# Attention logits in two row halves of the array, with the key sums and the mask in a bias tile made on GpSimd

## The chip, the cores and the metric

The kernel runs on one core of one Trainium2 chip. The metric is device time in microseconds of one launch. A profiled execution has a span (from the first to the last instruction of the program) and a time of its own, which is a little longer.

## What is computed

A small decoder trunk of two layers for 256 tokens of width 1024: a recurrent layer (RG-LRU), then an attention layer, each with two half-step feed-forward networks (hidden width 2816) around it and RMS norms. All data are float32. The part that matters here is the attention, with 16 heads of width 64 and a running sum `c` of forget gates per head and token:

```python
log_f = jax.nn.log_sigmoid((hn @ w_f + b_f).astype(jnp.float32))
c = jnp.cumsum(log_f, axis=1).transpose(0, 2, 1)
...
logits = jnp.einsum('bhqd,bhkd->bhqk', q[:, :, q0:end], k[:, :, :end]).astype(jnp.float32)
logits = logits + c[:, :, q0:end, None] - c[:, :, None, :end]
logits = jnp.where(kpos[None, :] <= qpos[:, None], logits, -jnp.inf)
p = jax.nn.softmax(logits, axis=-1).astype(v.dtype)
```

## The kernel before

The 256 tokens are two row tiles of 128, called `t` = 0 and 1. Every matrix product runs as three products in fp32r (a 32-bit format of TensorE): each weight tile is loaded (`raw`), split on ScalarE into an upper part `whi` (line 173) and on VectorE into the rest `wlo` (line 177), and `mm3` (lines 183 to 185) adds hi x hi, hi x lo and lo x hi into a PSUM bank `mm`. Weights come through a list of items in the order of use. An item has a `prep` (load and split) and a `work` for each row tile. Up to nine split items lie ready, so the preps run ahead of the work. `ahead(i, fn)` runs a function just before the prep of item `i`; `defer(n, fn)` runs one after `n` more steps of work.

The program order on TensorE is written by hand. VectorE, ScalarE, GpSimd (POOL) and the DMA queues are ordered by the framework's scheduler, which takes instructions under `high_priority` first and keeps the order only of those marked `keep_in_program_order`.

Stages in order: feed-forward, recurrent layer, feed-forward, keys and values with the forget gates (`post_f`, `running`), feed-forward of layer 2 (its first four items run ahead of the keys and values), attention, feed-forward. Inside a feed-forward network a gate tile `sil` and a product `prod` are made for 512 hidden columns at a time. A DMA on the SP queue moves `prod` to a tile `prr` (line 515), and TensorE transposes that some steps later (line 525). The last 256 columns (`alone`) take `prr` from the two buffers of tag `sil`. The 22 down-projection items follow.

Logits before: queries and keys are stored transposed, one head at a time, in `qT` and `kT` with 66 rows: 64 of the head, and two that carry the sums, so that one product over 66 rows gives q.k + c(query) - c(key). `heads_T` transposes two heads at once and copies the lower 64 rows with ScalarE and the upper 64 with VectorE, so that both start at row 0. In float32 a product takes two passes in the trace.

The attention stage is a hand-written order, `ATT_ORDER` (line 1125). A digit is one half-item of the projections for that row tile. A letter with a digit is a step of the attention for that row tile: `l` logits of one group (four heads at t=0 with 128 keys, two at t=1 with 256 keys; one 512-wide bank of tag `gt`, which has two), `n` normalisation, `t` transposes of the probabilities (line 1084), `v` the product with the values in two column halves (line 1098). In `l`, TensorE makes the logits (line 1063), VectorE adds the causal mask (1064) and takes the negated maximum (1066), and ScalarE takes the exponential with a row sum (1071). In `n`, VectorE inverts the sum (1077) and multiplies (1078). There are four groups at t=0 and eight at t=1.

Of the kernel before, what the change touches and what calls it, by code (L numbers as in the profile page):

```python
# [23 lines left out]
NRT = 11  # L24
NH = 16
HD = 64
HA = HD + 2
EPS = 1e-6
RAW = 5
WB = 9  # L30
# [3 lines left out]
NEG = -1e30  # L34
# [10 lines left out]
def trunk_kernel(ctx: ExitStack, tc: tile.TileContext, A: dict, out: bass.AP):  # L45
    nc = tc.nc
# [5 lines left out]
    hpool = ctx.enter_context(tc.tile_pool(name="h", bufs=1))  # L52
    spool = ctx.enter_context(tc.tile_pool(name="small", bufs=4))
    psum = ctx.enter_context(tc.tile_pool(name="psum", bufs=1, space=bass.MemoryType.PSUM))

    uid = [0]

    def nm(s):
        uid[0] += 1
        return f"{s}_{uid[0]}"  # L60
# [20 lines left out]
    def defer(n, fn):  # L81
        pend.append([n, fn])
# [474 lines left out]
    def std_dests(gi):  # L557
        return lambda t: [main_dest(gi, t)]


    pools = {}
# [345 lines left out]
    kv = {}  # L907
# [9 lines left out]

    def kv_tiles():
        lp = ctx.enter_context(tc.tile_pool(name="kv", bufs=1, reuse_waits="tile"))
        kv["kT"] = lp.tile([HA, NH, S], F32, name="kT")  # L920
# [3 lines left out]
        kv["c"] = [lp.tile([NH, P], F32, name=f"c{t}") for t in range(2)]  # L924
        kv["bfb"] = lp.tile([P, NH], F32, name="bfb")
        for n in ("triu", "mone", "cmask"):
            kv[n] = lp.tile([P, P], F32, name=n)

    def kv_constants():

        keep = tc.keep_in_program_order
        triu, cm = kv["triu"], kv["cmask"]
        keep(nc.gpsimd.dma_start(kv["bfb"], A["b_fgate"].partition_broadcast(P)))
        keep(nc.gpsimd.memset(triu, -1.0))
        keep(nc.gpsimd.affine_select(out=triu, in_=triu, compare_op=ALU.is_ge, fill=0.0, base=0,
                                     pattern=[[1, P]], channel_multiplier=-1))
        keep(nc.gpsimd.memset(kv["mone"], -1.0))
        keep(nc.gpsimd.memset(cm, 0.0))
        keep(nc.gpsimd.affine_select(out=cm, in_=cm, compare_op=ALU.is_ge, fill=NEG, base=0,
                                     pattern=[[-1, P]], channel_multiplier=1))  # L940
        keep(nc.gpsimd.memset(kv["kT"][HD:HA, :, :], 1.0))

    def att_rows():

        tc.keep_in_program_order(nc.scalar.activation(warm, mhalf, AF.Exp))
        for t in range(2):
            tc.keep_in_program_order(nc.gpsimd.dma_start(att["q"][t][HD:HD + 1, :, :], kv["c"][t]))
            tc.keep_in_program_order(nc.gpsimd.dma_start(att["q"][t][HD + 1:HA, :, :], kv["mone"][:NH, :]))

    def heads_T(pool, ps, t, n, scale, dst):  # L950

        tok = pool.tile([P, 512], F32, tag="prod", name=nm("htok"), bufs=2)
        with tc.high_priority():
            nc.vector.tensor_scalar(tok, ps, rs[t][:, 0:1], scale, ALU.mult, ALU.mult)

        def turn():
            tp = trbank()
            for j in range(4):
                nc.tensor.transpose(tp[:, j * P:(j + 1) * P], tok[:, j * P:(j + 1) * P], ident)  # L959
            to = dst[:HD, 8 * n:8 * n + 8, :].rearrange("p (a two) b -> p a two b", two=2)  # L960
            with tc.high_priority():
                nc.scalar.activation(to[:, :, 0, :], tp[:HD, :].rearrange("p (a b) -> p a b", a=4), AF.Copy)
                nc.vector.tensor_copy(to[:, :, 1, :], tp[HD:, :].rearrange("p (a b) -> p a b", a=4))
        defer(2, turn)

    def post_k(n):
        return lambda t, ps: heads_T(pools["f"], ps, t, n, 1.0, kv["kT"][:, :, t * P:(t + 1) * P])

    def post_f(t, ps):
        fp = pools["f"]  # L970
# [60 lines left out]
    for n in range(2):  # L1031
# [3 lines left out]
    ffn_items(lambda: pools["f"], A["ffn1_w_gate"][1], A["ffn1_w_up"][1], A["ffn1_w_down"][1], A["ffn1_post_g"][1],  # L1035
              std_dests(GI[("mix", 1)]))
    n_ffn3 = len(items)

    items[n_ffn2:n_kv + 4] = items[n_kv:n_kv + 4] + items[n_ffn2:n_kv]


    att = {}

    def att_tiles():
        ap = pools["a"]
        att["q"] = [ap.tile([HA, NH, P], F32, name=f"qT{t}") for t in range(2)]
        att["oh"] = [ap.tile([P, 8, P], F32R, name=f"oh{t}") for t in range(2)]
        att["ol"] = [ap.tile([P, 8, P], F32R, name=f"ol{t}") for t in range(2)]

    def attention(t):  # L1050

        ap = pools["a"]
        nk = t + 1
        per = 4 // nk
        mask = kv["cmask"].unsqueeze(1).to_broadcast([P, per, P])
        box = {}
        G = NH // per

        def logits(hg):
            hds = range(hg * per, (hg + 1) * per)  # L1060
            ps = gtbank().rearrange("p (a b) -> p a b", a=per)
            for j, hd in enumerate(hds):
                nc.tensor.matmul(ps[:, j, :], att["q"][t][:, hd, :], kv["kT"][:, hd, :nk * P], start=True, stop=True)  # L1063
            nc.vector.tensor_tensor(ps[:, :, t * P:], ps[:, :, t * P:], mask, ALU.add)
            mx = spool.tile([P, 4], F32, tag="mx", name=nm("mx"))
            nc.vector.tensor_reduce(mx[:, :per], ps, AX.X, ALU.max, negate=True)
            if hds[0] % 8 == 0:
                box["sm"] = spool.tile([P, 8], F32, tag="sm", name=nm("sm"))
            pe = ap.tile([P, per, nk * P], F32, tag="pe", name=nm("pe"), bufs=3)
            for j, hd in enumerate(hds):  # L1070
                nc.scalar.activation(pe[:, j, :], ps[:, j, :], AF.Exp, bias=mx[:, j:j + 1],
                                     accum_out=box["sm"][:, hd % 8:hd % 8 + 1])
            box["pe", hg], box["s", hg] = pe, box["sm"][:, hds[0] % 8:hds[0] % 8 + per]

        def norm(hg):
            pe, sm = box["pe", hg], box["s", hg]
# [30 lines left out]
        return {c: [lambda i=i, f=f: f(i) for i in range(G)] for c, f in zip("lntv", (logits, norm, turn, values))}  # L1107

    def post_q(n):
        return lambda t, ps: heads_T(pools["a"], ps, t, n, HD ** -0.5, att["q"][t])  # L1110

    for n in range(2):
        proj_items(A["attn_w_q"][0], n * 512, 512, main_x, post_q(n))
# [246 lines left out]
```

## Time and profile before

| | |
|---|---|
| median of 3 runs | 987.58 us (987.57 to 987.7) |
| the profiled execution | 987.51 us |
| its span | 985.8 us |
| TensorE busy | 978.0 us, 99% |
| VectorE busy | 616.6 us, 63% |
| ScalarE busy | 530.1 us, 54% |
| GpSimd busy | 47.2 us, 5% |
| attention stage, first to last logits | about 734 to 777 us |

A row of the page or of the groups names the line, the engine, the operation, what is written and read (`out<-in`), the shapes and the count, then busy time in us and mean ns of one, then the idle time ahead of it. In a timeline a row has the start in us, the length in us, and then the same names; several neighbours are merged, with their count. PE is TensorE, PEld its weight load, DVE VectorE, ACT ScalarE, POOL GpSimd, SP the engine that issues most DMAs. A matmul's length includes its way through the array, so the distance from one start to the next says what it costs in a stream.

### The profile page before, as it was taken

The page shows a single profiled execution, that of the slowest core. Times are in us where ns is not written, and L with a number is a line of the kernel's source. Part 1 is how long each engine was busy: PE and PEld are TensorE (multiplying, and loading weights), DVE is VectorE, ACT ScalarE, POOL GpSimd, SP SyncE. Part 2 cuts the span into 40 slices and gives each one's busy share as a digit, 9 for nine tenths or more (in the row PEclk, how much of TensorE's full clock was granted, in tenths as well). Part 3 has the DMA queues.
Part 4 walks back from the last instruction along what each step waited for, and adds up shares of the span by engine and source line. Part 5 has one row for each costly group of instructions (what it writes and reads, how often), then busy time and mean ns, then how long its engine had stood idle before and what let it go on. Part 6 is the DMA issues. An engine that isn't in the chain of part 4 may idle for free.

```text
span 985.8 us, 13028 instructions
## 1 busy us (share of the span) xinstructions
PE 978.0 (99%) x4777; PEld 813.4 (83%) x4777; DVE 616.6 (63%) x791; ACT 530.1 (54%) x753; POOL 47.2 (5%) x92
## 2 busy tenths in 40 slices
PE   9999999999999999999999999999999999999997
PEld 6888888898978888888898888888888788888886
DVE  6666554678997555554686655554488876555542
ACT  7545443568986544443564444544366755444431
POOL 2400000100003000000100000000020000000000
PEclk9999999999999999999999999999999999999999
DMA  8787766565346877666567676665552467776631
GB/s 292 263 266 249 222 210 192 158 192 162 117 126 198 241 211 212 217 207 188 131 203 242 186 220 213 214 213 185 190 173 64 123 210 235 213 213 212 205 117 43
DMA packets 99558, 190.45 MB, mean 193 GB/s; under 512 B 12734, under 2 KB 32614, under 8 KB 99494
## 3 DMA queue, kind: packets, MB, share of 16 engines
q1 hardware_dynamic: 98054, 188.95, 61.3%
q8 instruction: 38, 0.62, 0.3%
q10 hardware_dynamic: 608, 0.53, 0.2%
q0 software_dynamic: 832, 0.12, 0.1%
q14 instruction: 26, 0.21, 0.1%
HBM read 176.95 MB, written 1.05 MB: 181 GB/s over the span
## 4 chain that ended last, share of the span: by engine, by line
PE 98%; issue 1%; DVE 1%; ACT 0%; POOL 0%; POOLq 0%; DVEq 0%; ACTq 0%
PE mm L183 29%; PE mm L185 29%; PE mm L184 28%; PE gt L761 2%; PE tr L525 1%; PE mm L1195 1%; PE gt L1063 1%; PE mm L190 1%; PE mm L191 1%; PE mm L192 1%; PE mm L1098 1%; PE tr L1084 1%; PE gt L214 1%; PE tr L127 0%; PE tr L959 0%
## 5 line engine op out<-in xcount | busy, mean ns | idle before, releaser
L177 DVE TENSOR_TENSOR wlo<-raw,whi 128x1024 fp32r<-128x1024 f32 (+5 forms) x329 | 395.3, 1207 | 268.3 <-ACT whi L173 266.1
L173 ACT ACTIVATE whi<-raw 128x1024 fp32r<-128x1024 f32 (+5 forms) x329 | 341.9, 1046 | 314.8 <-PE mm L185 260.2
L183 PE MATMUL mm<-whi,xhi 128*128 128x512 f32 (+1 forms) x768 | 301.2, 392 | 0.0
L185 PE MATMUL mm<-whi,xlo 128*128 128x512 f32 (+1 forms) x768 | 298.2, 388 | 0.3 <-DVE xlo L228 0.3
L184 PE MATMUL mm<-wlo,xhi 128*128 128x512 f32 (+1 forms) x768 | 297.9, 388 | 0.0
L185 PEld LDWEIGHTS mm<-whi,xlo 128*128 128x128 f32 x768 | 144.2, 188 | 30.7 <-DVE xlo L228 0.7
L183 PEld LDWEIGHTS mm<-whi,xhi 128*128 128x128 f32 x768 | 144.2, 188 | 29.4 <-issue 1.3
L184 PEld LDWEIGHTS mm<-wlo,xhi 128*128 128x128 f32 x768 | 144.3, 188 | 28.2 <-DVE wlo L177 0.3
L183 PE MATMUL mm<-whi,hhi 128*128 128x512 f32 x352 | 137.9, 392 | 0.0
L185 PE MATMUL mm<-whi,hlo 128*128 128x512 f32 x352 | 137.1, 389 | 0.0
L184 PE MATMUL mm<-wlo,hhi 128*128 128x512 f32 x352 | 137.0, 389 | 0.0
L185 PEld LDWEIGHTS mm<-whi,hlo 128*128 128x128 f32 x352 | 66.1, 188 | 13.9
L184 PEld LDWEIGHTS mm<-wlo,hhi 128*128 128x128 f32 x352 | 66.1, 188 | 13.3
L183 PEld LDWEIGHTS mm<-whi,hhi 128*128 128x128 f32 x352 | 66.1, 188 | 13.3
L510 DVE SCALAR_TENSOR_TENSOR prod<-mm,rstd,sil 128x512 f32<-128x512 f32 (+1 forms) x48 | 33.8, 705 | 35.2 <-PE mm L185 31.1
L498 ACT ACTIVATE sil<-mm,rstd 128x512 f32<-128x512 f32 (+1 forms) x48 | 31.2, 651 | 38.7 <-PE mm L185 34.2
L198 POOL TENSOR_SCALAR nv<-ss 128x1 f32<-128x1 f32 x22 | 9.6, 435 | 716.3 <-ACT junk L205 716.3
L529 ACT ACTIVATE hhi<-tr 128x512 fp32r<-128x512 f32 (+1 forms) x48 | 24.8, 558 | 13.8 <-PE tr L525 13.8
L205 ACT ACTIVATE junk<-mm 128x512 bf16<-128x512 f32 x24 | 14.3, 595 | 32.7 <-PE mm L185 32.6
L272 DVE TENSOR_TENSOR t<-mm,gb 128x512 f32<-128x512 f32 x24 | 16.1, 685 | 24.7 <-ACT junk L205 24.6
L530 DVE TENSOR_TENSOR hlo<-tr,hhi 128x512 fp32r<-128x512 f32 (+1 forms) x48 | 29.2, 640 | 2.6 <-ACT hhi L529 2.6
L183 PE MATMUL mm<-whi,zhi 128*128 128x340 f32 (+2 forms) x80 | 28.2, 353 | 0.0
(196 smaller groups left out, 885.8 us busy)
## 6 DMA issues: line engine op xcount, KB each, us to landing
raw<-in_ffn_w_down_dram SPq DMA_DIRECT2D x88, 512.0 KB
raw<-in_ffn_w_up_dram SPq DMA_DIRECT2D x80, 512.0 KB
raw<-in_ffn_w_gate_dram SPq DMA_DIRECT2D x78, 512.0 KB
prr<-prod SPq DMA_DIRECT2D x40, 256.0 KB
raw<-in_rg_w_in_dram SPq DMA_DIRECT2D x10, 504.0 KB
raw<-in_rg_w_out_dram SPq DMA_DIRECT2D x10, 504.0 KB
raw<-in_ffn_w_gate_dram SPq DMA_DIRECT2D x19, 256.0 KB
raw<-in_ffn_w_up_dram SPq DMA_DIRECT2D x16, 256.0 KB
```

Source lines behind the costliest of these rows:

```text
L173: up = nc.scalar.activation(hi[:parts, c:c + m], rawv[:, c:c + m], AF.Copy)
L177: nc.vector.tensor_tensor(lo[:parts, c:c + m], rawv[:, c:c + m], hi[:parts, c:c + m].bitcast(F32), ALU.subtract)
L183: nc.tensor.matmul(ps, xh, wh, start=first, stop=False)
L184: nc.tensor.matmul(ps, xh, wl, start=False, stop=False)
L185: nc.tensor.matmul(ps, xl, wh, start=False, stop=last)
L205: nc.scalar.activation(junk[:, :src.shape[1]], src, AF.Square, scale=f, accum_out=acc)
L272: nc.vector.tensor_tensor(t1[n], pf[n], gb[:, n * 512:(n + 1) * 512], ALU.mult)
L498: nc.scalar.activation(s[:, :nn], ps, AF.Silu, scale=rs[t][:, 0:1])
L510: nc.vector.scalar_tensor_tensor(pr[:, :nn], ps, rs[t][:, 0:1], s, ALU.mult, ALU.mult)
L529: nc.scalar.activation(hv, tp[:, :nn], AF.Copy)
L530: nc.vector.tensor_tensor(lv, tp[:, :nn], hv.bitcast(F32), ALU.subtract)
L761: nc.tensor.matmul(ps[j][:w, g * S:(g + 1) * S], wv[rows, o:o + w], xc[rows, k, :], start=start, stop=stop, skip_group_check=True)
```

## The change

- Queries and keys keep two heads per tile, in rows 0 to 63 and 64 to 127; one ScalarE copy replaces the two copies. The two extra rows go.
- One `l` step makes two groups at once into both `gt` banks, even heads into one and odd heads into the other; every second `l` step does nothing. `ATT_ORDER` stays.
- The key sums and the mask come as a bias tile per query, key and head. Its rows are written to DRAM, read back spread over 128 partitions and masked by a GpSimd select. For t=0 the tile stays on the chip (`bias0`). For t=1 it is built in DRAM, in four pieces that pass through tiles of tag `sil` while the down projection's weights are loaded, and is loaded (2 MB) at the start of the attention.
- One VectorE instruction per head adds logits and bias, writes the negated sum to `pe` and takes its minimum, in place of mask and maximum. The query sum is added to that and taken away again by two narrow operations. ScalarE takes the exponential from `pe`.
- `running` also makes the sums with queries on partitions (`cq`), by further products.
- The `htok` tiles of the queries take buffers of tag `pT`.

```diff
     def att_rows():
         tc.keep_in_program_order(nc.scalar.activation(warm, mhalf, AF.Exp))
-        for t in range(2):
-            tc.keep_in_program_order(nc.gpsimd.dma_start(att["q"][t][HD:HD + 1, :, :], kv["c"][t]))
-            tc.keep_in_program_order(nc.gpsimd.dma_start(att["q"][t][HD + 1:HA, :, :], kv["mone"][:NH, :]))
+        tc.keep_in_program_order(nc.gpsimd.dma_start(att["bias1"], kv["bias1"]))
+    def only_earlier(v):
+        tc.keep_in_program_order(
+            nc.gpsimd.affine_select(out=v, in_=v, compare_op=ALU.is_ge, fill=NEG, base=0,
+                                    pattern=[[0, 4], [-1, P]], channel_multiplier=1))
+    def key_rows(v, h0, nh, k):
+        tc.keep_in_program_order(nc.gpsimd.dma_start(v, kv["rows"][h0:h0 + nh, k * P:(k + 1) * P].partition_broadcast(P)))
+    def bias_rows(i):
+        def f():
+            if i == 0:
+                key_rows(kv["bias1"][:, :, :P], 0, NH, 0)
+            v = parts_of_bias[i] = pools["f"].tile([P, 512], F32, tag="sil", name=nm("bp"), bufs=2).rearrange(
+                "p (a b) -> p a b", a=4)
+            key_rows(v, 4 * i, 4, 1)
+        return f
+    def bias_part(i):
+        def f():
+            v = parts_of_bias.pop(i)
+            only_earlier(v)
+            tc.keep_in_program_order(nc.gpsimd.dma_start(kv["bias1"][:, 4 * i:4 * i + 4, P:], v))
+        return f
...
             with tc.high_priority():
-                nc.scalar.activation(to[:, :, 0, :], tp[:HD, :].rearrange("p (a b) -> p a b", a=4), AF.Copy)
-                nc.vector.tensor_copy(to[:, :, 1, :], tp[HD:, :].rearrange("p (a b) -> p a b", a=4))
+                nc.scalar.activation(dst[:, 4 * n:4 * n + 4, :], tp.rearrange("p (a b) -> p a b", a=4), AF.Copy)
...
     def running(t):
-        pc = gtbank()
+        pc, pq = gtbank(), gtbank()
+        one = kv["one"].to_broadcast([P, P])
         if t == 1:
-            nc.tensor.matmul(pc[:NH, :P], kv["lf"][0], kv["mone"], start=True, stop=False)
+            nc.tensor.matmul(pc[:NH, :P], kv["lf"][0], one, start=True, stop=False)
         nc.tensor.matmul(pc[:NH, :P], kv["lf"][t], kv["triu"], start=t == 0, stop=True)
-        nc.vector.tensor_copy(kv["c"][t], pc[:NH, :P])
-        nc.gpsimd.dma_start(kv["kT"][HD + 1:HA, :, t * P:(t + 1) * P], kv["c"][t])
+        if t == 1:
+            nc.tensor.matmul(pq[:, :NH], one, kv["lf"][0], start=True, stop=False)
+        nc.tensor.matmul(pq[:, :NH], kv["triu"], kv["lf"][t], start=t == 0, stop=True)
+        ct = pools["f"].tile([NH, P], F32, name=f"c{t}")
+        nc.vector.tensor_copy(ct, pc[:NH, :P])
+        nc.vector.tensor_copy(kv["cq"][t], pq[:, :NH])
+        nc.gpsimd.dma_start(kv["rows"][:, t * P:(t + 1) * P], ct)
+        if t == 0:
+            for h0 in range(0, NH, 4):
+                v = kv["bias0"][:, h0:h0 + 4, :]
+                key_rows(v, h0, 4, 0)
+                defer(30 + h0, lambda v=v: only_earlier(v))
...
+    for i in range(4):
+        ahead(n_ffn3 - 18 + 4 * i, bias_rows(i))
+        ahead(n_ffn3 - 15 + 4 * i, bias_part(i))
...
         def logits(hg):
-            hds = range(hg * per, (hg + 1) * per)
-            ps = gtbank().rearrange("p (a b) -> p a b", a=per)
-            for j, hd in enumerate(hds):
-                nc.tensor.matmul(ps[:, j, :], att["q"][t][:, hd, :], kv["kT"][:, hd, :nk * P], start=True, stop=True)
-            nc.vector.tensor_tensor(ps[:, :, t * P:], ps[:, :, t * P:], mask, ALU.add)
-            mx = spool.tile([P, 4], F32, tag="mx", name=nm("mx"))
-            nc.vector.tensor_reduce(mx[:, :per], ps, AX.X, ALU.max, negate=True)
...
+            if hg % 2:
+                return
+            h0 = hg * per
+            ps = [gtbank() for _ in range(2)]
+            def logit(hd):
+                j = (hd - h0) // 2
+                return ps[hd % 2][:, j * w:(j + 1) * w]
+            for hd in range(h0, h0 + 2 * per):
+                r = slice(hd % 2 * HD, (hd % 2 + 1) * HD)
+                nc.tensor.matmul(logit(hd), att["q"][t][r, hd // 2, :], kv["kT"][r, hd // 2, :w], start=True, stop=True,
+                                 skip_group_check=True)
...
+            for g in (hg, hg + 1):
+                hds = range(g * per, (g + 1) * per)
+                mx = spool.tile([P, 4], F32, tag="mx", name=nm("mx"))
+                pe = ap.tile([P, per, w], F32, tag="pe", name=nm("pe"), bufs=3)
+                for j, hd in enumerate(hds):
+                    nc.vector.tensor_tensor_reduce(pe[:, j, :], logit(hd), bias[:, hd, :], -1.0, -NEG, ALU.add, ALU.min,
+                                                   mx[:, j:j + 1])
+                cq = kv["cq"][t][:, h0 + (g - hg) * per:h0 + (g - hg) * per + per]
+                nm_q = spool.tile([P, 4], F32, tag="nmq", name=nm("nmq"))
+                nc.vector.tensor_tensor(nm_q[:, :per], mx[:, :per], cq, ALU.add)
+                nc.vector.tensor_tensor(nm_q[:, :per], nm_q[:, :per], cq, ALU.subtract)
+                for j, hd in enumerate(hds):
+                    nc.scalar.activation(pe[:, j, :], pe[:, j, :], AF.Exp, bias=nm_q[:, j:j + 1], scale=-1.0,
+                                         accum_out=box["sm"][:, hd % 8:hd % 8 + 1])
```

More of the change, by code (lines that the diff above doesn't have):

```diff
@@ L925, in kv_tiles @@
         kv["bfb"] = lp.tile([P, NH], F32, name="bfb")
-        for n in ("triu", "mone", "cmask"):
-            kv[n] = lp.tile([P, P], F32, name=n)
+        kv["triu"] = lp.tile([P, P], F32, name="triu")
+        kv["one"] = lp.tile([P, 32], F32, name="one")[:, :1]
+        kv["bias0"] = lp.tile([P, NH, P], F32, name="bias0")
+        kv["rows"] = dram.tile([NH, S], F32, name="crows")
+        kv["bias1"] = dram.tile([P, NH, S], F32, name="bias1d")
     def kv_constants():
         keep = tc.keep_in_program_order
-        triu, cm = kv["triu"], kv["cmask"]
+        triu = kv["triu"]
@@ new lines, in trunk_kernel @@
+    parts_of_bias = {}
+    def bias_rows(i):
[12 more added lines that the diff above has]
+        return f
@@ L953, in heads_T @@
+    def heads_T(pool, ps, t, n, scale, dst, tag, bufs):
+        tok = pool.tile([P, 512], F32, tag=tag, name=nm("htok"), bufs=bufs)
         with tc.high_priority():
@@ L1045, in att_tiles @@
         ap = pools["a"]
-        att["q"] = [ap.tile([HA, NH, P], F32, name=f"qT{t}") for t in range(2)]
+        att["q"] = [ap.tile([P, NH // 2, P], F32, name=f"qT{t}") for t in range(2)]
+        att["bias1"] = ap.tile([P, NH, S], F32, name="bias1")
         att["oh"] = [ap.tile([P, 8, P], F32R, name=f"oh{t}") for t in range(2)]
@@ L1054, in attention @@
         per = 4 // nk
-        mask = kv["cmask"].unsqueeze(1).to_broadcast([P, per, P])
+        bias = kv["bias0"] if t == 0 else att["bias1"]
+        w = nk * P
         box = {}
```

29 lines of the change are left out of this document (9 added, 20 removed).

## The prediction

> **What bounds the kernel now.** I read the page first: the engines, the chain that ended last, then the groups; after it the windows and the timeline of the attention stage, and last the places that the new work would sit beside.
>
> ```profile
> span 985.8 us, 13028 instructions
> PE 978.0 (99%) x4777; PEld 813.4 (83%) x4777; DVE 616.6 (63%) x791; ACT 530.1 (54%) x753; POOL 47.2 (5%) x92
> PE 98%; issue 1%; DVE 1%; ACT 0%; POOL 0%; POOLq 0%; DVEq 0%; ACTq 0%
> ACT whi L173 <- PE mm L185: 260.2, 186, 3.3
> ACT whi L173 <- DMA raw<-in_ffn_w_up_dram: 10.0, 9, 1.8
> ```
>
> TensorE is 98% of the chain. The two waits say who is early: the weight split waits 260.2 us for a split buffer that TensorE has yet to release, and 10.0 us for the largest of the loads. So weights are ready ahead of time, and what counts is what TensorE itself spends, plus any place where it would newly wait. The changed stage, in three windows (PE, PEld, DVE, ACT, POOL busy; clock; DMA):
>
> ```profile
> 745.00:753.00 8.00, 7.99 (x57) 6.51 (x56) 6.77 (x11) 4.95 (x20) 0.00 (x0) 1.00 0.42 129
> 753.00:763.00 10.00, 10.00 (x61) 7.86 (x60) 6.86 (x15) 5.26 (x18) 0.00 (x0) 1.00 0.00 0
> 763.00:773.00 10.00, 10.00 (x65) 8.01 (x66) 9.82 (x17) 8.69 (x17) 0.00 (x0) 1.00 0.45 125
> ```
>
> No idle TensorE, the clock at 1.00, and VectorE between 6.86 and 9.82 of 10: it is the next in line.
>
> **The logits on TensorE, before.** The timeline of PE (start, length, engine, line, tiles, count) around four logits blocks:
>
> ```profile
> 734.65 1.11 PE L1063 MATMUL gt<-kT,qT 66*128 66x128 f32 x8
> 735.52 0.47 PE L183 MATMUL mm<-whi,xhi 128*128 128x512 f32 x1
> 735.83 0.39 PE L184 MATMUL mm<-wlo,xhi 128*128 128x512 f32 x1
> 736.06 0.39 PE L185 MATMUL mm<-whi,xlo 128*128 128x512 f32 x1
> 744.23 1.05 PE L1063 MATMUL gt<-kT,qT 66*128 66x128 f32 x8
> 745.21 0.66 PE L1098 MATMUL mm<-pT,v 128*64 128x128 f32 x8
> 753.01 1.03 PE L1063 MATMUL gt<-kT,qT 66*128 66x256 f32 x4
> 753.97 0.66 PE L1098 MATMUL mm<-pT,v 128*64 128x128 f32 x8
> 759.47 1.03 PE L1063 MATMUL gt<-kT,qT 66*128 66x256 f32 x4
> 760.34 0.60 PE L1084 MATMUL tr<-ident,pe 128*128 128x128 f32 x4
> ```
>
> Each float32 product is two passes. A block for t=1 costs 760.34 - 759.47 = 0.87 us, or 0.217 a pass. The one ahead of the value products takes 753.97 - 753.01 = 0.96, so entering the column halves of L1098 costs 0.09 more. A block for t=0 takes 744.23 to 745.21, 0.98, or 0.89 without that 0.09; its eight passes alone are 735.52 - 734.65 = 0.87, 0.11 each. Before: 4 x 0.89 + 8 x 0.87 = 10.5 us on the path.
>
> **The logits, after.** Two heads stand in rows 0 to 63 and 64 to 127 and write different banks. The gates of the recurrent layer already do just that:
>
> ```profile
> 220.85 2.95 PE L761 MATMUL gt<-xc,gw 126*126 126x256 f32 x16
> 222.67 0.73 PEld L761 LDWEIGHTS gt<-xc,gw 64*126 64x126 f32 x8 [0.33 <-issue]
> 223.73 0.19 PEld L183 LDWEIGHTS mm<-whi,xhi 128*128 128x128 f32 x1 [0.33 <-issue]
> 223.73 0.50 PE L183 MATMUL mm<-whi,xhi 128*128 128x512 f32 x1
> 224.07 0.39 PE L184 MATMUL mm<-wlo,xhi 128*128 128x512 f32 x1
> ```
>
> Of these 16 passes, 8 over all rows take 220.85 to 222.67, 1.82 us; at 0.217 they would take 1.73, so 0.09 is lost going into halves. Eight half-row passes follow, all issued within 0.73 us, and the next product starts at 223.73: 1.06 us. Four paired passes at 0.217 are 0.87; one after another the eight would be 1.73, so the halves do overlap. The other 0.19 is about half the first exposed weight load and half the way back out. Then L183 to L184 takes 0.34, against 0.23 in the stream at 735.83 and 736.06 (0.11 of a load not hidden). A visit thus costs 0.09 + 1.06 + 0.11 = 1.26 with full-array work on both sides, and about 1.06 where column-half products follow, which pay for leaving full mode already.
>
> The Trainium skill, TensorEngine Tiling (Array Packing), section Key Properties, speaks against many short visits: it says that changing the tiling mode, rather than only the tile, drains TensorE. The trace agrees, with 0.09 to 0.10 us at each change; taken without the drain, the page's "up to 2x" would give 5.2 us for the six visits.
>
> After: six visits with the work of two blocks each (8 paired passes at 0.11 or 4 at 0.217, about 0.87 either way). By the written order the first (t=0) and the fourth (t=1, ahead of transposes) have full-array work on both sides, 2 x 1.27; the other four run into value products, 4 x 1.07. Sum 6.8, so 10.5 - 6.8 = **3.7 us saved**. Bounds: 5.3 saved if no switch cost anything, 2.9 if all six pay both ends.
>
> **The query sums.** `running` gains one product at t=0 and two at t=1, six passes that load 128 columns and stream 16. The nearest rows are the 128-column passes above at 0.11, bound by the load as much as by the stream: **0.66 us added** on the path (bounds 0.4 and 0.9).
>
> **The softmax chain.** VectorE and ScalarE by shape (busy, mean ns):
>
> ```profile
> L1066 DVE TENSOR_REDUCE mx<-gt 128x2 f32<-128x512 f32 x8 | 5.5, 682 | 0.0
> L1064 DVE TENSOR_TENSOR gt<-gt,cmask 128x256 f32<-128x256 f32 x8 | 3.4, 422 | 0.9 <-PE gt L1063 0.8
> L285 DVE SCALAR_TENSOR_TENSOR h<-t,rstd,h 128x256 f32<-128x256 f32 x4 | 1.7, 480 | 0.1
> L833 DVE TENSOR_TENSOR_SCAN tt<-th,tt 126x256 f32<-126x256 f32 x10 | 6.2, 668 | 0.0
> L249 DVE SCALAR_TENSOR_TENSOR xlo<-gt,gT,xhi 128x128 fp32r<-128x128 f32 x16 | 4.5, 340 | 0.4 <-ACT xhi L246 0.4
> L1077 DVE RECIPROCAL sm<-sm 128x2 f32<-128x2 f32 x8 | 1.3, 160 | 1.7 <-ACT pe L1071 1.7
> L963 DVE COPY qT<-tr 64x512 f32<-64x512 f32 x4 | 2.8, 693 | 1.7 <-ACT qT L962 1.6
> 750.31 0.69 DVE L1078 TENSOR_TENSOR pe<-pe,sm 128x512 f32<-128x512 f32 x1
> 751.15 0.63 PE L1084 MATMUL tr<-ident,pe 128*128 128x128 f32 x4
> ```
>
> Mask and maximum cost VectorE 0.42 + 0.68 = 1.10 us per group at t=1. The new add-and-minimum over 256 columns isn't in the trace; it lies between L285 (0.48) and the scan (0.67). I take 0.48, since it makes one result per element as L285 does. Two of them and two narrow operations at 0.16 make 1.28: 0.18 more per group, 0.56 by the scan. At t=0 four at 0.34 and the narrow pair make 1.68; a 512-wide mask and maximum, at 0.69 and 0.69 like L1078 and L1066, make 1.38; so 0.30 more. Eight and four groups: +2.6, or +5.7 by the scan; the four qT copies that go give back 2.8. VectorE's total hardly moves, and ScalarE's exponentials keep their count. What moves is the order: both groups' maxima come at once, and the odd block that stood between an even group's logits and its transposes is gone, so that group has 0.87 us less. The tightest is the third: its normalisation ends at 751.00 and its transposes start at 751.15. It is short by up to 0.15 - 0.87 - 0.30, about -1.0; part comes back because the qT copy no longer stands in its way. I take **0.5 us of new waiting** (bounds 0 and 2.5).
>
> **The bias tiles.** All of it is issued from POOL, busy for 47.2 us of the span:
>
> ```profile
> L935 POOL TENSOR_SCALAR_AFFINE_SELECT triu<-triu 128x128 f32<-128x128 f32 x1 | 1.0, 990 | 0.1
> kT<-c POOLq DMA_DIRECT2D x2, 8.0 KB, 4.5
> 726.05 0.58 POOL L947 DMA_DIRECT2D qT<-c  x1
> 728.74 1.02 POOL L198 TENSOR_SCALAR nv<-ss 128x1 f32<-128x1 f32 x1 [0.68 <-ACT junk L205]
> 720.00:730.00 10.00, 10.00 (x50) 8.38 (x49) 10.00 (x13) 8.50 (x14) 4.05 (x8) 1.00 0.82 292
> ```
>
> Eight selects over 512 columns, at most 4 x 0.99 each, and 16 transfers in place of six, at 0.58 of issue like the small one at 726.05: costed at nothing, since apart from the row statistics nobody waits for POOL, and by the written order the selects lie in the kv stage's aftermath and among the down loads, between two of these. The 2 MB load takes the place of the four small ones at 726.05; at 292 GB/s it needs 7.2 us, shared half and half 14.4, so it lands by 741, and t=1's first logits come near 751.7 (753.01 less 1.3). Were that cover gone, each us past 752 would be lost one for one. Behind it on POOL stands the 728.74 statistic, which four issues preceded before and one does now. About 6 MB of extra traffic shares the queues with weights that wait on TensorE anyway.
>
> Sum against the profiled execution: 985.8 - 3.7 + 0.66 + 0.5 = 983.3 of span. That run took 987.51, 1.7 outside the span: 985.0. The median of the runs, 987.58, lies 0.07 above it: **985.1 us**.
>
> **The rivals.** *VectorE takes it back.* The Trainium skill's tiling page, section PSUM Bottleneck, says that tiling speeds up TensorE but not the emptying of PSUM. As a mechanism of this kernel: with the scan's price, the first and third groups lose about 1 us each and one later group 0.5, in all 2.5, so 985.1 + 2.0 = 987.1. For it: 9.82 of 10 in the third window. Against: 6.8 and 6.9 in those before.
>
> *A bias piece holds up the last hidden block (slower).* The pieces take buffers of tag sil, which has two; the last up-projection's prr comes from the same two. SP, then PE:
>
> ```profile
> 658.05 0.47 SPq L515 DMA_DIRECT2D prr<-prod  x1
> 660.32 6.56 SPq L164 DMA_DIRECT2D raw<-in_ffn_w_down_dram  x3
> 663.96 0.29 PE L525 MATMUL tr<-identr,prr 128*128 128x128 f32 x2
> ```
>
> The move at 658.05 feeds transposes at 663.96, 5.9 us later. A piece is given back only after its select and its way out. If prr gets that buffer, it waits until the piece's part runs among the down loads that start at 660.32, say at 663, plus 4.0 for the select and 4.5 for the way out: to about 671; TensorE then waits some 7 us, and the weight loads behind it on SP too. Result about 992. It decides from 5.9 us of delay on. Against it: prr can take the buffer of its own sil, which is read out just before. Which one it gets isn't in this trace.
>
> *The bias load is late*, past 754: about 988. *The halves don't overlap* in this shape, so the change doesn't do what it says: six more blocks, 985.1 + 5.2 = 990.3; L761 speaks against it.
>
> **How the numbers follow.** Forecast 0.50, VectorE 0.28, held block 0.12, late load 0.05, no overlap 0.05. A measurement can tell about 0.2%, 2 us, so faster means below 985.6. Of the forecast's 0.50 about 0.43 lies there and 0.07 within; VectorE gives 0.03 faster and 0.25 within; the late load is within for 0.03. That makes 0.46, 0.35 and 0.19. The forecast's own range is 983.9 (switches that cost less) to 986.2; for 8 in 10 it goes to the VectorE case's end and the late load, 989.2.
>
> **What would show it.** The logits lines with six visits, two heads starting together, about 1.1 to 1.3 us each; three products more in `running`; PE still gapless ahead of the transposes. Wrong would be: PE waiting for the normalisation at the first and third groups, prr issued late near 664, or add-and-minimum above 0.67 us.

## The result and the profile after

The changed kernel takes 993.82 us (median of 6 runs, 993.42 to 994.21) against 987.64 us of the kernel before, a ratio of 1.0058 with a 95% interval of 1.0045 to 1.0071: 6.2 us slower where 2.5 us faster was forecast. The page of the profiled execution (994.21 us):

```profile
span 992.5 us, 13106 instructions
PE 983.1 (99%) x4783; PEld 809.9 (82%) x4783; DVE 610.4 (61%) x849; ACT 530.9 (53%) x753; POOL 58.5 (6%) x107
PE 94%; DVE 2%; issue 1%; ACT 1%; POOL 0%; POOLq 0%; DVEq 0%; ACTq 0%
```

TensorE is busy for 983.1 us, 5.1 more than the 978.0 before, with less logits work to do. So most of the loss isn't waiting: something goes slower. I laid the two traces side by side by the n-th large product and looked where their distance grows. It grows evenly in stages that the diff doesn't touch. The first down-projection, long before any attention work, by its first product and the first product behind its last; the kernel before, then after:

```profile
136.55 0.39 PE L183 MATMUL mm<-whi,hhi 128*128 128x512 f32 x1
...
193.43 0.39 PE L183 MATMUL mm<-whi,xhi 128*128 128x512 f32 x1
```

```profile
137.46 0.40 PE L183 MATMUL mm<-whi,hhi 128*128 128x512 f32 x1
...
195.69 0.39 PE L183 MATMUL mm<-whi,xhi 128*128 128x512 f32 x1
```

56.88 us became 58.23. The groups by line and shape say the same (count, busy us, mean ns); the kernel before:

```profile
L183 PE MATMUL mm<-whi,xhi 128*128 128x512 f32 x752 | 296.2, 394 | 0.0
L183 PE MATMUL mm<-whi,hhi 128*128 128x512 f32 x352 | 137.9, 392 | 0.0
```

and after:

```profile
L183 PE MATMUL mm<-whi,xhi 128*128 128x512 f32 x752 | 296.0, 394 | 0.0
L183 PE MATMUL mm<-whi,hhi 128*128 128x512 f32 x352 | 139.8, 397 | 0.0
```

A product whose stationary operand is `hhi` takes 5 ns more, one with `xhi` doesn't. Start to start the median goes from 227 to 232 ns, for `hhi`, `hlo`, `zhi`, `zlo` and `y` alike. There are 1,272 such products of 512 columns (1,056 with `hhi` or `hlo`, 96 with `zhi` or `zlo`, 120 with `y`), and five nanoseconds on each make 6.4 us. The granted clock over this stage is 1.00 in both.

The attention stage itself did become shorter, from 71.18 to 69.45 us (from the first query product to the first product of the last feed-forward block), but with three waits, where the kernel before has one of 0.08 us. Logits, values and transposes on PE after:

```profile
747.84 0.63 PE L1138 MATMUL tr<-ident,pe 128*128 128x128 f32 x4 [0.47 <-DVE pe L1132]
751.15 1.16 PE L1109 MATMUL gt<-kT,qT 64*128 64x128 f32 x16
752.24 0.66 PE L1152 MATMUL mm<-pT,v 128*64 128x128 f32 x8
...
757.67 0.63 PE L1138 MATMUL tr<-ident,pe 128*128 128x128 f32 x4 [0.40 <-DVE pe L1132]
...
759.62 1.13 PE L1109 MATMUL gt<-kT,qT 64*128 64x256 f32 x8
...
765.43 1.14 PE L1109 MATMUL gt<-kT,qT 64*128 64x256 f32 x8
766.50 0.66 PE L1138 MATMUL tr<-ident,pe 128*128 128x128 f32 x4
...
784.37 0.63 PE L1138 MATMUL tr<-ident,pe 128*128 128x128 f32 x4 [0.72 <-DVE pe L1132]
```

A visit of logits for two groups takes 766.50 - 765.43 = 1.07 us, or 1.09 at t=0 (752.24 - 751.15), as the recurrent gates had shown. The transposes of the first, third and eleventh group wait for VectorE's normalisation; start to start these waits are 0.63, 0.47 and 0.79 us, beyond the distance that the same step has elsewhere in this trace (0.11 us behind other transposes, 0.20 behind value products). The ends of products are modelled, so the idle time in brackets is shorter.

### The profile page after: what moved, and what is told of

Same layout as the page of the kernel before. It is cut to its first block, busy times and chain, and to the rows that moved or that the text cites. A ratio compares the mean times of both kernels' runs of the same rounds, so it can differ in the third digit from the quotient of the medians.

```text
span 992.5 us, 13106 instructions
## 1 busy us (share of the span) xinstructions
PE 983.1 (99%) x4783; PEld 809.9 (82%) x4783; DVE 610.4 (61%) x849; ACT 530.9 (53%) x753; POOL 58.5 (6%) x107
## 4 chain that ended last, share of the span: by engine, by line
PE 94%; DVE 2%; issue 1%; ACT 1%; POOL 0%; POOLq 0%; DVEq 0%; ACTq 0%
PE mm L183 28%; PE mm L185 28%; PE mm L184 28%; PE gt L761 2%; PE tr L525 1%; PE mm L1249 1%; PE mm L190 1%; PE mm L191 1%; PE mm L192 1%; DVE wlo L177 1%; ACT pe L1125 1%; PE gt L214 1%; DVE pe L1118 0%; PE tr L127 0%; PE gt L1109 0%
```

## The experiments

**Where the 5 ns come from.** The diff adds one small tile to the pool `small`, `nmq`, four buffers of 16 bytes, which take 32 bytes each: 128 bytes. The pool lies in front of every pool that holds stationary operands other than `xhi`. By the addresses that the two builds assign, the split weights (the moving operand) stand at 160 modulo 256 in both kernels, and so do `xhi` and `xlo`; `hhi`, `zhi`, `y` and their lower halves stand at 160 before and at 32 after. Two operands whose addresses are equal modulo 256 are called level below. Theory 1 is that this placement costs the 5 ns; theory 2 that the new work or its transfers do.

*Realigned.* One number of the changed kernel is altered, so that the four buffers take 256 bytes in place of 128:

```diff
-                nm_q = spool.tile([P, 4], F32, tag="nmq", name=nm("nmq"))
+                nm_q = spool.tile([P, 16], F32, tag="nmq", name=nm("nmq"))
```

> The kernel after, with the new small tile made 64 bytes instead of 16: four buffers of it take 256 bytes in front of all later tiles instead of 128, nothing else changes. Theory 1 (placement): the down-projections and the other products whose stationary operand stands behind that tile go at 232 ns instead of 227 because of where that operand stands; put 128 bytes further on, they go at 227 again, 1240 of them times 5 ns is 6.2 us, so about 987.6 us, and the four down stages last 56.9 us each as in the kernel before. Theory 2 (the new work itself, its transfers or GpSimd, slows the products): the stages stay at 58.2 to 58.4 us and the time at 993.8.

Measured: 986.67 us (11 runs, 986.07 to 987.15), ratio 0.9989 to the kernel before (0.998 to 0.9997). The row of its groups is that of before:

```profile
L183 PE MATMUL mm<-whi,hhi 128*128 128x512 f32 x352 | 137.9, 392 | 0.0
```

The four down stages last 56.89, 56.89, 56.89 and 55.76 us; theory 2 is out. 7.15 us come back where 6.2 were expected, because 5 ns is the step of the median: by the mean of the distances from start to start (those under 0.3 us) the `hhi` and `hlo` products take 232.8 ns in the changed kernel and 226.9 here. The four down stages give 5.8 us of it (the table below), the stages of the products with `y`, `zhi` and `oh` 0.46, 0.42 and 0.18.

*The kernel before, shifted.*

```diff
-            mx = spool.tile([P, 4], F32, tag="mx", name=nm("mx"))
+            mx = spool.tile([P, 16], F32, tag="mx", name=nm("mx"))
```

> The kernel before, with the small tile of the maxima made 64 bytes instead of 16, so that everything behind it stands 128 bytes further on; no instruction changes. Theory 1 (placement): all four down stages go from 56.9 to about 58.3 us, the products from 227 to 232 ns, and the time from 987.6 to about 994. Theory 2 (the new work): nothing changes, 987.6.

Measured: 995.14 us, ratio 1.0077 (1.0061 to 1.0092). No instruction differs from the kernel before, and the loss is there:

```profile
L183 PE MATMUL mm<-whi,xhi 128*128 128x512 f32 x752 | 296.2, 394 | 0.0
L183 PE MATMUL mm<-whi,hhi 128*128 128x512 f32 x352 | 139.8, 397 | 0.0
```

*Everything shifted.* Is it the address itself, or where the one operand stands against the other?

```diff
-    gT = cpool.tile([P, 56], F32, name="gT")
+    gT = cpool.tile([P, 88], F32, name="gT")[:, :56]
```

> The kernel after, with 128 bytes put in front of the weights' buffers, so that weights, xhi and all later tiles move together by 128 bytes. If it is the place of the stationary operand alone that counts, the down-projections go at 227 ns and the many products with xhi, now moved too, at 232: 2250 of them times 5 ns is 11 us more, about 999 us. If what counts is how the stationary operand stands to the moving weights, nothing changes: down-projections at 232, products with xhi at 227, 993.8 us. If it is the new work, also 993.8.

Measured: 993.35 us (2 runs), the changed kernel's time. `hhi` is now at 160 modulo 256, the place that was fast, but the weights are at 32, and the rows are still these:

```profile
L183 PE MATMUL mm<-whi,xhi 128*128 128x512 f32 x752 | 296.1, 394 | 0.0
L183 PE MATMUL mm<-whi,hhi 128*128 128x512 f32 x352 | 139.8, 397 | 0.0
```

*Weights against both.* The last one leaves open what the hidden activations have to stand level with. This kernel moves the weights by 128 bytes and all behind them by 256:

```diff
-    gT = cpool.tile([P, 56], F32, name="gT")
+    gT = cpool.tile([P, 88], F32, name="gT")[:, :56]
...
+    hpool.tile([P, 32], F32, name="spacer")
     h = [hpool.tile([P, D], F32, tag=f"h{t}", name=f"h{t}") for t in range(2)]
```

> The kernel after, with 128 bytes in front of the weights' buffers and 128 more in front of the residual and xhi: weights move by 128, xhi and the hidden activations by 256. Modulo 256 the weights then stand level with hhi, hlo, zhi, zlo, y and oh, and 128 bytes away from xhi and xlo. If it is the place of the stationary operand against the moving weights that counts, the pattern turns over: the down stages go at 56.9 us, and the long stages of products with xhi take 2% more, 104.1 to about 106.4 and 120.0 to about 122.5 us; some 2250 products times 5 ns make 11 us, so about 998. If the place against something else counts (xhi, the residual, PSUM), the down stages stay at 58.3 and the stages with xhi at 104.1 and 120.0: 993.8.

Measured: 998.3 us (2 runs), ratio 1.0108 (1.0089 to 1.0126), and the pattern turns over (line numbers are one higher here):

```profile
L184 PE MATMUL mm<-whi,xhi 128*128 128x512 f32 x752 | 299.8, 399 | 0.0
L184 PE MATMUL mm<-whi,hhi 128*128 128x512 f32 x352 | 137.9, 392 | 0.0
```

*Other offsets*, in the kernel before, one for each pool of hidden activations:

```diff
+    PAD = {"ffn_a": 16, "ffn_b": 48, "ffn_c": 8}
+
     def open_pool(key, name):
         cm = tc.tile_pool(name=name, bufs=1, reuse_waits="tile")
         pools[key] = cm.__enter__()
+        if name in PAD:
+            pools[key].tile([P, PAD[name]], F32, name="pad")
```

> The kernel before, with a spacer at the head of three of the pools that hold the hidden activations: the first feed-forward block's moves by 64 bytes, the second's and third's by 192, the last's by 32. Placement theory: 0 and 256 bytes give 227 ns and 128 gives 232. If only the bit of 128 bytes counts, 64 and 32 bytes give 56.9 us of down stage (the addresses 224 and 192 modulo 256 have it as 160 has) and 192 bytes, address 96, gives 58.3. If any offset between the two operands costs, all four stages are slower than 56.9. If the cost grows with the offset, the stage at 32 bytes is the nearest to 56.9.

A single run: 993.3 us. Offsets of 32, 64 and 192 bytes cost too, so it isn't the bit of 128 bytes, and 32 isn't the mildest. Stage lengths in us, worked out from the unrounded starts of the first product of a stage and the first behind it, in down 4 of its last product (in brackets, how far the stationary operand stands from the weights modulo 256):

| stage | before | after | realigned | before shifted | all shifted | offsets | weights against both |
|---|---|---|---|---|---|---|---|
| down 1 | 56.89 (0) | 58.22 (128) | 56.89 (0) | 58.45 (128) | 58.41 (128) | 58.47 (64) | 56.89 (0) |
| down 2 | 56.89 (0) | 58.25 (128) | 56.89 (0) | 58.24 (128) | 58.25 (128) | 57.41 (192) | 56.91 (0) |
| down 3 | 56.87 (0) | 58.42 (128) | 56.89 (0) | 58.24 (128) | 58.25 (128) | 58.26 (192) | 56.91 (0) |
| down 4 | 55.79 (0) | 57.34 (128) | 55.76 (0) | 57.34 (128) | 57.14 (128) | 57.35 (32) | 55.78 (0) |
| gate and up 3 (444 products) | 104.10 (0) | 104.08 (0) | 104.10 (0) | 104.08 (0) | 104.06 (0) | 104.09 (0) | 106.43 (128) |

Level costs nothing, every other offset tried costs 1 to 3%. That the second and third stage differ at the same 192 bytes isn't explained. The place of the stationary operand against the moving weights is thus shown as the cause, from both sides: moved out of level in a kernel whose instructions are unchanged, and moved back. Weights and hidden activations stood at 160 and 160 modulo 256 (realigned), 160 and 32 (changed), 32 and 160 (all shifted), 32 and 32 (weights against both): both level places are fast and both others slow. What inside TensorE it disturbs was not tried.

**Where the forecast gain went.** The realigned kernel shows the change without the placement: 1.0 us faster than before, where 2.5 were forecast. Three waits stand in it, 0.63, 0.47 and 0.83 us by the same measure (what was expected of the runs below takes 0.11 us off each, and so has 0.57 and 0.93 for the last two). VectorE's timeline of the changed kernel around the first of them:

```profile
742.66 0.29 DVE L1118 CUSTOM_DVE_ANT_0 pe<-gt,bias 128x128 f32<-128x128 f32 x1 [3.24 <-PE gt L1109]
...
743.72 0.16 DVE L1122 TENSOR_TENSOR nmq<-mx,cq 128x4 f32<-128x4 f32 x1
743.80 0.28 DVE L1118 CUSTOM_DVE_ANT_0 pe<-gt,bias 128x128 f32<-128x128 f32 x1
744.25 0.75 DVE L978 TENSOR_SCALAR htok<-mm,rstd 128x512 f32<-128x512 f32 x1 [0.16 <-PE mm L185]
744.92 0.15 DVE L1123 TENSOR_TENSOR nmq<-nmq,cq 128x4 f32<-128x4 f32 x1
...
746.79 0.18 DVE L1131 RECIPROCAL sm<-sm 128x4 f32<-128x4 f32 x1 [0.90 <-ACT pe L1125]
747.00 0.69 DVE L1132 TENSOR_TENSOR pe<-pe,sm 128x512 f32<-128x512 f32 x1
```

The first group's four maxima are made by 743.6. Its bias for the exponential needs two more narrow operations; the second stands behind the other group's work and a wide query copy and starts at 744.92. The exponentials follow, the normalisation is done at 747.69, the transposes run at 747.84. Theory W1 is that this extra hop costs the time, W2 that two groups' maxima at once fill VectorE.

*Without the narrow pair.* (Query sums are added to the maximum and subtracted again; a softmax doesn't depend on what is taken off its row.)

```diff
-                cq = kv["cq"][t][:, h0 + (g - hg) * per:h0 + (g - hg) * per + per]
-                nm_q = spool.tile([P, 16], F32, tag="nmq", name=nm("nmq"))
-                nc.vector.tensor_tensor(nm_q[:, :per], mx[:, :per], cq, ALU.add)
-                nc.vector.tensor_tensor(nm_q[:, :per], nm_q[:, :per], cq, ALU.subtract)
...
-                    nc.scalar.activation(pe[:, j, :], pe[:, j, :], AF.Exp, bias=nm_q[:, j:j + 1], scale=-1.0,
+                    nc.scalar.activation(pe[:, j, :], pe[:, j, :], AF.Exp, bias=mx[:, j:j + 1], scale=-1.0,
```

> The realigned kernel without the two narrow VectorE operations per group (query sums added to the maximum and taken off again); the exponential takes the maximum itself as its bias, which leaves the weights of the softmax as they are. Three groups of transposes wait for their normalisation in the realigned kernel, 0.63, 0.57 and 0.93 us, 2.1 in all. Theory W1 (the extra hop): the pair's second operation comes 1.4, 0.3 and 1.1 us after its group's last maximum, behind a wide query copy, another group's maxima or an attention output; without it the exponentials start that much earlier, the waits fall to about 0.3 us in all and the time from 986.7 to about 984.9. Theory W2 (two groups' maxima at once and the weight splits in between fill VectorE): the waits stay near 1.8 and the time near 986.4.

Measured: 985.27 us, ratio 0.9979 (0.997 to 0.9988), between the two theories' times and nearer to W1's. In its mechanism W1 holds: of TensorE's waits for the normalisation (idle us in all, times, longest; first the changed kernel's row) none is left. A new one, for the copy of transposed weights on ScalarE, has come (second row), 0.73 us from start to start. The 1.93 us of waiting that go, less these 0.73, make 1.20. The attention stage gets 1.14 us shorter (69.27 to 68.13), and the medians differ by 1.40:

```profile
PE tr L1138 <- DVE pe L1132: 1.6, 3, 0.7
```

```profile
PE mm L1148 <- ACT pT L1136: 0.6, 1, 0.6
```

*Odd groups at their own place.*

```diff
-            if hg % 2:
-                return
-            h0 = hg * per
-            ps = [gtbank() for _ in range(2)]
+            h0 = hg // 2 * 2 * per
+            if hg % 2 == 0:
+                box["ps"] = [gtbank() for _ in range(2)]
+            ps = box["ps"]
...
-            for hd in range(h0, h0 + 2 * per):
+            for hd in range(h0, h0 + 2 * per) if hg % 2 == 0 else ():
...
-            for g in (hg, hg + 1):
+            for g in (hg,):
...
```

> The realigned kernel, in which the odd group's maxima, pair and exponentials are issued at the odd group's own place in the written order, as before, while TensorE still makes both groups' logits at the even one's. Theory W2: with only one group's maxima ahead of the normalisation, the first and the last wait (0.63 and 0.93 us) mostly go, about 985.3. Theory W1: the pair still comes late behind whatever else VectorE has, the waits change by less than 0.5 us in all, about 986.5. Against it: the bank pair is held longer, so a visit of logits may wait for it, up to 1 us.

Measured: 996.23 us, 9.6 more than the realigned kernel; both theories missed. The eight maxima of the first two groups still run close together, from 736.37 to 738.9, but both pairs now come behind them and the exponentials behind a weight split on ScalarE. TensorE waits 4.10, 2.86 and 2.19 us. With the first two waits its clock falls to half, each time for 3.41 us, and with the third it doesn't. Below are stretches of 3.41 us, each a whole number of them from the first fall at 744.38 (busy us and counts of PE, PEld, DVE, ACT, POOL; granted clock; DMA). The third wait lies across the fifth and sixth row:

```profile
740.97:744.38 3.41, 0.12 (x2) 0.00 (x0) 1.91 (x5) 3.41 (x16) 0.00 (x0) 1.00 0.49 142
744.38:747.79 3.41, 2.77 (x9) 2.41 (x10) 1.72 (x2) 1.10 (x2) 0.00 (x0) 0.50 0.26 50
754.61:758.02 3.41, 1.16 (x13) 0.75 (x11) 2.04 (x5) 2.87 (x12) 0.00 (x0) 1.00 0.00 0
758.02:761.43 3.41, 2.87 (x9) 2.52 (x10) 0.39 (x1) 0.60 (x1) 0.00 (x0) 0.50 0.00 0
778.50:781.91 3.41, 2.60 (x27) 1.61 (x25) 3.41 (x13) 3.07 (x10) 0.00 (x0) 1.00 0.84 271
781.91:785.32 3.41, 2.10 (x13) 1.82 (x14) 3.35 (x10) 2.27 (x6) 0.00 (x0) 1.00 0.88 312
785.32:788.74 3.42, 3.42 (x31) 2.68 (x30) 2.33 (x7) 2.03 (x9) 0.00 (x0) 1.00 0.51 136
```

*Both edits.*

> Both edits: no narrow pair, and the odd group's maxima at the odd group's place. W1: about 984.9, no better than without the pair alone. W2: as with the odd groups moved alone, about 985.3. If the two causes add, no wait above 0.2 us is left ahead of the transposes: 986.7 less 2.0, about 984.7.

Measured: 985.77 us (0.9982, 0.9973 to 0.9991), no better than without the pair alone. A wait of 1.10 us is left in t=0 and one of 0.31 in t=1. The first part of the attention stage is worse than without the pair alone (33.34 us against 32.27), the second better (35.47 against 35.86).

*No query sums*, on top of both edits. The 128 bytes of the sums' tiles are added to the tile `one`, so that nothing behind it moves:

```diff
-            nc.tensor.matmul(pq[:, :NH], one, kv["lf"][0], start=True, stop=False)
-        nc.tensor.matmul(pq[:, :NH], kv["triu"], kv["lf"][t], start=t == 0, stop=True)
...
-        nc.vector.tensor_copy(kv["cq"][t], pq[:, :NH])
```

> As the kernel with both edits, and without the query sums, which nothing reads any more: three products of two passes less in the first stage of keys and values (0.67 us measured there for them), two copies less on VectorE. About 0.7 us less than the kernel with both edits, near 984.1, the stage of the zhi products back from 38.45 to 37.8 us. If those products lay beside other work, no change.

Measured: 985.58 us. The stage falls from 38.45 to 37.80 us as said, but 0.45 us was lost again elsewhere in the profiled execution. Its row on ScalarE, and the one on PE that follows from it:

```profile
659.86 0.47 ACT L498 ACTIVATE sil<-mm,rstd 128x256 f32<-128x256 f32 x1 [3.56 <-DMA bias1d<-bp]
```

```profile
664.33 0.37 PE L525 MATMUL tr<-identr,prr 128*128 128x128 f32 x2 [0.28 <-DVE hlo L530]
```

The activation of the last hidden block waited 3.56 us for a buffer of tag `sil` that a bias piece still held, and the move `prr`, issued 2 us later than in the next kernel, reached its transposes 0.45 us late. In the changed kernel the same wait was 1.10 us, and no PE wait followed from it:

```profile
662.56 0.47 ACT L498 ACTIVATE sil<-mm,rstd 128x256 f32<-128x256 f32 x1 [1.10 <-DMA bias1d<-bp]
```

*No pair, no query sums*, odd groups as in the change:

> The realigned kernel without the narrow pair and, since nothing reads them then, without the query sums: the edits of the kernel without the pair and of the one without query sums together, with the odd groups where the change put them. If the two are independent: 985.27 less 0.67 (the stage of the zhi products from 38.45 to 37.8 us), about 984.6, and 3.0 us under the kernel before. If the query sums lay beside other work in this version, 985.3.

Measured: 984.77 us (7 runs), ratio 0.9971 (0.996 to 0.9982), as added up.

*One product moved*, against the wait that was left:

```diff
-"... n1 l1 t1 0 n1 v1 v1 t1 0 t1 1 v1 v1 1 1 1 1 1 1 1"
+"... n1 l1 t1 0 n1 0 v1 v1 t1 1 t1 v1 v1 1 1 1 1 1 1 1"
```

> The same, with one product of the first row block moved ahead of the value products that wait, and one of the second row block ahead of the last transposes but one. The one wait left in the kernel without the pair, 0.72 us inside the value products of the second t=1 output half but one, stands behind the copy of the transposed weights on ScalarE. If a product of 1.3 us in front covers it, about 0.6 us less than without this edit, 984.0. If ScalarE is late by more, or the transposes that follow now wait for their normalisation, no gain or up to 0.5 us more, 984.6 to 985.1.

Measured: 987.22 us, 2.5 worse. The product that was moved forward is the last of its row block, so that block's closing work on ScalarE and VectorE (its squares, residual and norm) now stands in front of the last copy of transposed weights. TensorE waits for 1.94 us from start to start (1.77 idle), and its clock falls to half in the stretch of 3.41 us that begins at 781.85:

```profile
781.67 0.98 PE L1143 MATMUL mm<-pT,v 128*64 128x128 f32 x8 [1.77 <-ACT pT L1131]
```

```profile
778.44:781.85 3.41, 1.64 (x18) 1.10 (x18) 1.42 (x2) 1.87 (x4) 0.55 (x2) 1.00 0.00 0
781.85:785.26 3.41, 3.41 (x14) 2.55 (x13) 1.83 (x2) 1.30 (x2) 0.24 (x1) 0.50 0.13 18
```

*Odd groups later for t=1 alone*, no pair, no query sums:

```diff
-            if hg % 2:
+            if hg % 2 and t == 0:
                 return
...
-            for g in (hg, hg + 1):
+            for g in (hg, hg + 1) if t == 0 else (hg,):
...
```

> No pair and no query sums, realigned, and the odd group's maxima and exponentials at the odd group's own place for t=1 alone; for t=0 both groups together as in the change. In the traces the first part of the attention stage (before the first oh product) is shortest with both together, 32.27 us against 33.34, and the second with the odd groups later, 35.47 us against 35.86. If the two parts are independent, 32.27 + 35.47 = 67.7 us of stage, 0.4 less than the kernel with no pair and no sums, about 984.4 us. If the order in the second part depends on how the first leaves VectorE's queue, no gain, 984.8.

Measured: 984.62 us (6 runs, 984.18 to 984.93), ratio 0.9969 (0.9957 to 0.9981), the lowest median of all. The two parts last 32.27 and 35.49 us, and 0.18 us of idle time before the copy is left. The gain over the kernel with no pair and no query sums, 0.35 us of stage, is within the spread of the runs. So no run bears W2 out: with the pair gone, moving the odd groups gained nothing that is clear of it.

## Why the prediction was wrong

The kernel got 6.2 us slower, beyond the range's end of 989.2, for a reason that no term, bound or rival held. **The step that failed is the sum itself: it priced every instruction that the change adds and no byte.** The tile of the narrow pair was counted as two operations at 0.16 us, not as 128 bytes in front of all hidden activations. That costs 7.15 us by the two medians, 993.82 less 986.67. The diff and the sizes of the tiles would have shown the shift; that it has a price could not be read from the trace of before, where all long products ran level. The held-up hidden block, with its 992 us, came nearest in number, but by luck: TensorE didn't wait for those transposes.

The other terms, read with the placement set right:

| term | forecast | measured |
|---|---|---|
| logits in halves | 10.5 to 6.8, -3.7 | from the starts on PE, 10.76 to 6.44 + 6 x 0.10 for going into halves, -3.7 |
| query sums | +0.66 | 38.45 - 37.78 = +0.67 |
| new waits | +0.5 (0 to 2.5) | 1.93 less the 0.08 of before, +1.85 |
| sum | -2.5 | -1.2 (runs: -1.05, realigned kernel) |

Both totals of the logits are 0.2 to 0.3 us above the forecast's, and the two misses cancel in the difference.

**Logits.** Six visits of 1.06 to 1.09 us with 0.10 for going into halves each, where 1.06 to 1.26 was said. The halves overlap; that rival is out.

**Query sums.** Six passes, two a product, on the path as costed; the realigned kernel's rows:

```profile
518.47 0.40 PE L1018 MATMUL gt<-lf,triu 128*128 128x16 f32 x2
...
531.03 0.39 PE L1017 MATMUL gt<-lf,one 128*128 128x16 f32 x2
531.28 0.37 PE L1018 MATMUL gt<-lf,triu 128*128 128x16 f32 x2
```

**The softmax chain** is the term of the sum that was mis-sized, 0.5 us where 1.85 came, inside its bounds. The price wasn't at fault: add-and-minimum is cheaper than said, 0.42 us for 256 columns and 0.29 for 128, where 0.48 and 0.34 stood:

```profile
L1118 DVE CUSTOM_DVE_ANT_0 pe<-gt,bias 128x256 f32<-128x256 f32 x16 | 6.2, 418 | 0.3 <-PE gt L1109 0.3
L1118 DVE CUSTOM_DVE_ANT_0 pe<-gt,bias 128x128 f32<-128x128 f32 x16 | 3.8, 285 | 3.2 <-PE gt L1109 3.2
```

The narrow pair was costed as 0.32 us of VectorE; it is two more places in a queue in which wide operations stand, and each place can cost what stands in front, up to 1.2 us (a weight split). The first and the third group wait, as named; the eleventh stands only in the VectorE rival, as "one later group". One row was misread as well. The 0.15 us from the end of the third group's normalisation to its transposes was counted as slack, but the same 0.15 stands in the changed kernel where TensorE does wait (747.00 + 0.69 to 747.84). In the kernel before, these transposes start 0.28 us after the last value product where the other groups' start 0.20 after, so that group had no slack and already waited 0.08 us. Taking the pair away gave back 1.4 us. So the rival in which VectorE takes the gain back (987.1) was closer than the forecast in its size, and its mechanism (a dear operation) was not the one that did it.

**A held-up hidden block** was placed in the right ring but at the wrong tenant: the piece holds up the `sil` of the last block, not its `prr`. In the changed kernel, where the wait is 1.10 us, the move is issued 5.54 us ahead of its transposes and nothing waits for it. With the wait of 3.56 us it was issued 2.90 us later than in the kernel before, counted from the `sil` of the preceding block, and 0.45 was lost. So about 2.4 us of delay were free, not the 5.9 that the prediction gave: that distance also holds the move and the splits themselves. **The bias load** is issued where it was said to be (732.60; the trace runs 6.7 us behind that of before at this place), 27 us ahead of the first t=1 logits at 759.62, lands 10.9 us after its issue, and VectorE's add-and-minimum waits for no transfer.

```profile
732.60 0.63 POOL L972 DMA_DIRECT2D bias<-bias1d  x1
```

## What to carry to other kernels

A change has a memory layout as well as instructions: list each tile it adds, drops or resizes, see which operands behind it move, and keep TensorE's stationary operands level with its moving ones (here modulo 256 bytes). If a stage that the diff doesn't touch gets slower by the same few nanoseconds per instruction, compare addresses before looking for contention, and shift the old kernel by the same bytes. And price a narrow operation in a dependent chain by what can stand in front of it in its queue, not by its own length.

## What was not expected of the hardware

Where the stationary operand stands against the moving one changes a float32r product of 512 columns from 227 to 232 ns start to start, 2.2%, at offsets of 32, 64, 128 and 192 bytes modulo 256 (one stage at 192 showed less, 57.41 us instead of 58.3). Products of 340 and 360 columns hardly noticed: their medians are 155 and 155, and 164 and 165 ns. The Trainium skill, TensorE: Matmul & The Clock Gate, section Step-by-step: what each phase is for, says that loading the next weights does not steal read bandwidth from the running matmul, because each has its own read port. Where the two operands stand level, nothing here speaks against that; out of level a product takes 5 ns more, and whether these are a collision of the two reads stays open.

The length of a wait alone doesn't decide whether TensorE's clock falls: one of 1.94 us did it, one of 2.19 us did not. In the kernel with the odd groups moved the two falls are 758.02 - 744.38 = 13.64 us apart, four times the 3.41 that each lasts, as if the clock were set anew every 3.41 us. In the stretches just before the three falls TensorE was busy for 0.12, 1.16 and 1.64 us; in the two that share the wait of 2.19 us it was busy for 2.60 and 2.10, and the clock stayed at 1.00. By these rows what counts is how much TensorE did within one such stretch; the limit would lie between 1.64 and 2.10 us, an estimate that no run was made to test. A fall is dear: products then take 427 ns instead of 227 for 3.41 us. By these figures that loses up to 1.6 us of work, an estimate, and makes the wait of 1.94 us nearly twice as dear. The Trainium skill, TensorE: Matmul & The Clock Gate, section What's actually happening, gives an idle window of about 3.4 us for the fall. The trace agrees on the length, 3.41 us. It doesn't agree if the window has to be free of work, since 1.64 us of work stood in one ahead of a fall, and the measurement decides.
